# A hybrid RG-LRU, attention and mixture-of-experts layer: an explicit TensorE order in the RG-LRU stage, gates alternating with eighths of a sigmoid block, adaLN sums left in the stage

## The chip, the core and the metric

The kernel runs on one core of one Trainium2 chip. Five engines work side by side and wait for each other by semaphores: TensorE (PE in the rows) multiplies matrices into PSUM, ScalarE (ACT) and VectorE (DVE) work on tiles, GpSimd (POOL) does the same more slowly and starts a few transfers, SyncE (SP) only issues DMA transfers. Each engine runs its own instructions strictly in order. The metric is the device time of one execution in microseconds, as the median of several.

## The reference

One layer for 1024 latent tokens and 256 context tokens, width 1024, in float32. Three branches share one input projection; the part that the change touches is the first.

```python
z_l = split(modulate(rmsnorm(x, g1), mod_l[0], mod_l[1]) @ w_in)      # also z_c from the context
xr  = centred_depthwise_conv(z_l[0], conv_w, conv_b)                  # width 4, per channel
for d, rev in ((0, False), (1, True)):                                # RG-LRU, both directions
    r, i  = sigmoid(xr @ wa[d] + ba[d]), sigmoid(xr @ wx[d] + bx[d])  # block diagonal, 8 blocks
    log_a = -8 * r * softplus(-lam[d])
    h[d]  = scan(exp(log_a), sqrt(-expm1(2 * log_a)) * (i * xr))      # starts from the context's state
rnn = (h[0] + h[1]) * gelu(z_l[1])
g   = sigmoid(z_l[5])                                                 # two gates of 1024 channels
merged = g[0] * (rnn @ w_rnn_out) + g[1] * (attention @ w_mla_out)
x_new  = x + mod_l[2] * (merged @ w_o)
out    = x_new + mod_l[5] * moe(modulate(rmsnorm(x_new, g2), mod_l[3], mod_l[4]))
mod_l  = split(silu(c) @ w_ada + b_ada, 6)                            # the adaLN sums
```

## The kernel before

A float32 product is done as three products of rounded parts (high by high, low by high, high by low), so that each weight and each activation exists as a pair of tiles: `wh`/`wl`, `xh`/`xl`, `xrh`/`xrl`, `rh`/`rl`. ACT casts the high part from the raw tile (`wr`), DVE subtracts for the low part.

The work goes in stages: the norm and the first adaLN sums, the projections for attention, then the **RG-LRU stage** (TensorE from about 265 to 588.5 us in the profiled execution), the product with `w_rnn_out` (tile `ro`), attention, the output projection, routing, and sixteen experts.

The RG-LRU stage goes over 8 blocks of 128 channels. For block b:

- `conv_part(b + 1)`: 48 matmuls of 512 columns (tile `z0`, printed `z` in the rows) and 24 of 256 columns for the context (`z0c`); ACT copies the sums out and DVE adds the three other taps (tile `xr`).
- `lru_part(b)`: four gates (r and i, two directions), each of 6 matmuls of 512 columns (`gz`) and 3 of 256 (`gc`), with ACT's sigmoid on each; then ACT's tanh (`vv`) and, after a load of another function table, exp (`av`). DVE squares (`r`), forms `vv`, and after ACT's square root `i`, then scans (`r`, three instructions), adds the directions and multiplies with the gelu tile (`ge`), which goes to memory (`rn_d`). GpSimd multiplies `i` with `xr`.
- `sig_block`: a block of the merge gates, 48 matmuls (`zg`), ACT's sigmoid (`sg`), and a store. `sig_plan` gives blocks 0 to 7 one, one, one, two, one, one, two and three of them.
- `mod_step`: one of 32 slices of the later adaLN rows. A slice of `w_ada` is loaded into a `wr` buffer and DVE adds it, scaled, into `acc`. Every eighth ends a row: TensorE sums `acc` over the partitions with a matrix of ones (`mp`, 4 matmuls), ACT copies the row (`g`), and it is stored.

In this stage the order of ACT is that of the code (a manual schedule); the orders of TensorE, DVE, GpSimd and SP are set by a scheduler. PSUM is eight banks: tag "a" has three buffers of two banks (`gz`, `z0`, `zg`, `mp`, later `ro`), tag "b" two of one bank (`z0c`, `gc`). `wr` buffers for weights, `w_ada` slices and reloaded `rn_d` rows come from one set of four.

In block 7 the three sig blocks come last. Around them `load_rn` begins to bring back the rows of `rn_d` and to split them (`rh`, `rl`) into memory that the stage's own tiles had held, and `ro` of the next stage multiplies them with `w_rnn_out`: 8 output blocks of 48 matmuls, k from 0 to 7 inside.

Of the kernel before, what the change touches and what calls it, by code (L numbers as in the profile page):

```python
# [19 lines left out]
F32 = mybir.dt.float32  # L20
# [40 lines left out]
def layer_kernel(ctx: ExitStack, tc: tile.TileContext, I, rope_tab, out, dbg=None):  # L61
# [269 lines left out]
    def nextw(shape):  # L331
        n = taken[0]
        assert items[n][1] == shape, (items[n], shape)
        taken[0] = n + LOOK
        fetch()
        taken[0] = n + 1
        return ahead[n]

    LOOK = 2
    NFIRST = 3  # L340
    MP2, N2 = 1, 0
# [38 lines left out]
    cur_pool = []  # L380

    def mpool():
        return cur_pool[-1]

    macc = {}

    def mod_step(j):
        m, k = divmod(j, KD)
        if k == 0:
            macc[m] = mpool().tile([P, D], F32, name="acc", bufs=1)  # L390
            nc.gpsimd.memset(macc[m], 0.0)
            nc.sync.dma_start(macc[m][0:1, :], I["b_ada"][:, (2 + m) * D:(3 + m) * D])
# [4 lines left out]
        if k == KD - 1:  # L397
            row = mpool().tile([1, D], F32, name="g", tag="sg", bufs=1)
            mp = pa("mp")
            for n in range(2):  # L400
                sl = slice(n * 512, (n + 1) * 512)
                nc.tensor.matmul(mp[0:1, sl], ones, acc[:, sl], start=True, stop=True)
            nc.scalar.copy(row, mp[0:1, :])
            nc.sync.dma_start(mod_d[m:m + 1, :], row)


    with pool("p2") as p2:
# [141 lines left out]
        cur_pool.append(p2)  # L549
# [9 lines left out]
        for j, i in enumerate(order):  # L559
            zp = qkv(i, *zp, lambda: zq(order[j + 1]) if j + 1 < len(order) else None)  # L560
            if fill:
                fill_block(*fill.pop(0))
            for _ in range(MP2):
                if steps and steps[0] < N2:
                    mod_step(steps.pop(0))


    p3c = pool("p3")
    p3 = p3c.__enter__()
    if True:  # L570
        p4c = None

        def sig_block(dst, mid=None):
            zz = pa("zg")
            zblock(zz)
# [9 lines left out]
        def conv_part(b):  # L585
            zc, zz = pb("z0c"), pa("z0")
# [8 lines left out]
            xrh = p3.tile([P, TOK], F32R, name="xrh", bufs=2)  # L595
            xrl = p3.tile([P, TOK], F32R, name="xrl", bufs=2)
            return xr, xrh, xrl

        def lru_part(b, xr, xrh, xrl):
            gh, gl_ = nextw([2, 2, P])  # L600
            gates = []
            for d in range(2):
                for g, bn in ((0, "ba"), (1, "bx")):
                    gc, gz = pb("gc"), pa("gz")
# [4 lines left out]
                    r = p3.tile([P, TOK], F32, name=("r", "i")[g], bufs=2)  # L609
# [4 lines left out]
            av, vv = [], []  # L614
            for d in range(2):
                v = p3.tile([P, TOK], F32, name="vv", bufs=2)
                nc.scalar.activation(v, gates[2 * d], AF.Tanh, scale=p8[:, d * 8 + b:d * 8 + b + 1])
                vv.append(v)
            for d in range(2):
# [8 lines left out]
            def rest():  # L628
# [17 lines left out]
                nc.sync.dma_start(rn_d[b], ge)  # L646

            return rest
# [3 lines left out]
        def load_rn(n=None):  # L652
            for k in range(len(rh), n or min(len(rh) + 2, KD - 1)):
# [7 lines left out]
        cur_pool.append(p3)  # L661
        with tc.manual_schedule(engines={mybir.EngineType.Activation}):
# [20 lines left out]
            split(nxt[1], nxt[2], nxt[0])  # L683
            for b in range(KD):
# [3 lines left out]
                rest = lru_part(b, *cur)  # L688
                if b + 1 < KD:
                    split(nxt[1], nxt[2], nxt[0])  # L690
                for n in range(sig_plan[b]):
                    w, bb = jobs.pop(0)
                    if b == KD - 1 and n == 1:
                        assert not steps
# [3 lines left out]
                    sig_block((s0_d, s1_d)[w][bb], rest if n == 0 else load_rn if b == KD - 1 else None)  # L698
                    for _ in range(4):
                        if steps:  # L700
                            mod_step(steps.pop(0))
            load_rn(KD)


    xnp.__exit__(None, None, None)
# [107 lines left out]
    for b in range(KD):  # L813
        h, l = nextw([KD, P])
        po = pa("ro")
        for k in range(KD):
            for n in range(2):
                sl = slice(n * 512, (n + 1) * 512)
                mm3(po[:, sl], h[:, k], l[:, k], rh[k][:, sl], rl[k][:, sl], k == 0, k == KD - 1)
        sg = p4.tile([P, SEQ], F32, name="s0", bufs=1)  # L820
# [460 lines left out]
```

## Time and profile before

| | |
|---|---|
| median of 3 executions | 1780.97 us (1778.66 to 1781.80) |
| profiled execution | 1780.6 us, span 1778.5 us |
| mean granted TensorE clock in it | 0.977 of full speed |
| TensorE busy | 1675.9 us, 94% of the span |
| VectorE busy | 1336.1 us, 75% |
| ScalarE busy | 992.9 us, 56% |

The span runs from the first to the last instruction of the profile; the rest of the execution's time lies around it. "Busy" of TensorE is modelled from the starts of its matmuls and their pipelined ends, so that neighbours overlap; how fast it goes is read from start to start. Idle time stands in brackets behind the instruction that it came before, with what ended it.

### The profile page before, as it was taken

The page shows a single profiled execution, that of the slowest core. Times are in us where ns is not written, and L with a number is a line of the kernel's source. Part 1 is how long each engine was busy: PE and PEld are TensorE (multiplying, and loading weights), DVE is VectorE, ACT ScalarE, POOL GpSimd, SP SyncE. Part 2 cuts the span into 40 slices and gives each one's busy share as a digit, 9 for nine tenths or more (in the row PEclk, how much of TensorE's full clock was granted, in tenths as well). Part 3 has the DMA queues.
Part 4 walks back from the last instruction along what each step waited for, and adds up shares of the span by engine and source line. Part 5 has one row for each costly group of instructions (what it writes and reads, how often), then busy time and mean ns, then how long its engine had stood idle before and what let it go on. Part 6 is the DMA issues. An engine that isn't in the chain of part 4 may idle for free.

```text
span 1778.5 us, 20714 instructions
## 1 busy us (share of the span) xinstructions
PE 1675.9 (94%) x7769; PEld 1345.5 (76%) x7769; DVE 1336.1 (75%) x1628; ACT 992.9 (56%) x1087; POOL 251.8 (14%) x188
## 2 busy tenths in 40 slices
PE   8999999999999999999999899909999999999996
PEld 3788888787777877777677678807888888888885
DVE  5755545898897554787876756687999999989995
ACT  3433325765677313667776532406777777777773
POOL 2123331111221100111110100000121111112101
PEclk9999999999999999999999999958999999999999
DMA  9264444445452854000000446567999999999971
GB/s 345 83 176 107 111 104 116 129 145 174 148 158 95 284 173 162 28 28 28 28 1 0 160 183 228 231 249 265 379 397 392 399 396 385 399 400 378 393 296 24
DMA packets 174179, 363.72 MB, mean 205 GB/s; under 512 B 40160, under 2 KB 90744, under 8 KB 174080
## 3 DMA queue, kind: packets, MB, share of 16 engines
q1 hardware_dynamic: 169472, 345.63, 53.6%
q0 software_dynamic: 4608, 16.78, 3.7%
q8 instruction: 61, 1.00, 0.2%
q14 instruction: 38, 0.31, 0.0%
HBM read 314.84 MB, written 47.54 MB: 204 GB/s over the span
## 4 chain that ended last, share of the span: by engine, by line
PE 63%; DVE 17%; issue 6%; ACT 6%; DMA 5%; POOL 3%; SPq 0%; POOLq 0%; DVEq 0%; ACTq 0%
PE w_e_gate L99 3%; PE w_e_gate L100 3%; PE w_e_gate L98 3%; PE w_e_down L99 3%; PE w_e_down L100 3%; PE w_e_down L98 3%; PE w_e_up L99 3%; PE w_e_up L98 3%; PE w_e_up L100 3%; PE pm L783 2%; POOL st L143 2%; PE xo L98 2%; PE s L98 2%; PE xo L100 2%; PE xo L99 2%
## 5 line engine op out<-in xcount | busy, mean ns | idle before, releaser
L95 DVE TENSOR_TENSOR el<-ma,eh 128x2048 fp32r<-128x2048 f32 x114 | 258.4, 2288 | 24.0 <-PE w_e_down L99 12.6
L94 ACT CAST eh<-ma 128x2048 fp32r<-128x2048 f32 x114 | 217.7, 1914 | 75.4 <-PE w_e_up L100 28.8
L95 DVE TENSOR_TENSOR el<-me,eh 128x2048 fp32r<-128x2048 f32 x78 | 176.9, 2288 | 18.9 <-PE w_e_gate L99 7.2
L94 ACT CAST eh<-me 128x2048 fp32r<-128x2048 f32 x78 | 148.9, 1914 | 49.8 <-PE w_e_gate L100 19.4
L847 ACT ACTIVATE pr<-s 128x512 f32<-128x512 f32 x160 | 95.6, 600 | 75.3 <-PE s L100 73.8
L785 DVE TENSOR_REDUCE mx<-pm 128x1 f32<-128x320 f32 x256 | 114.6, 484 | 23.4 <-PE pm L783 21.0
L99 PE MATMUL z<-xl,wh 128*128 128x512 f32 x320 | 126.6, 396 | 1.7 <-DVE xl L280 1.7
L100 PE MATMUL z<-xh,wl 128*128 128x512 f32 x320 | 126.3, 396 | 0.9 <-POOL wl L326 0.9
L98 PE MATMUL z<-xh,wh 128*128 128x512 f32 x320 | 126.4, 397 | 0.0
L1227 POOL DMA_INDIRECT out_dram<-y,icol x16 | 52.3, 3268 | 471.6 <-DVE y L1226 471.6
L94 ACT CAST wh<-wr 128x1024 fp32r<-128x1024 f32 (+1 forms) x53 | 52.0, 982 | 118.2 <-PE z L99 52.4
L95 DVE TENSOR_TENSOR pl<-pr,ph 128x1024 fp32r<-128x1024 f32 x64 | 81.3, 1271 | 31.5 <-ACT ph L94 24.8
L98 PE MATMUL w_e_gate<-eh,xgh 128*128 128x512 f32 x256 | 102.4, 400 | 1.1 <-ACT xgh L94 1.1
L99 PE MATMUL w_e_gate<-el,xgh 128*128 128x512 f32 x256 | 102.3, 400 | 0.0
L100 PE MATMUL w_e_gate<-eh,xgl 128*128 128x512 f32 x256 | 101.3, 396 | 0.2 <-DVE xgl L95 0.2
L99 PE MATMUL w_e_down<-el,hdh 128*128 128x512 f32 x256 | 101.5, 396 | 0.0
L98 PE MATMUL w_e_down<-eh,hdh 128*128 128x512 f32 x256 | 100.4, 392 | 1.1 <-ACT hdh L94 1.1
L99 PE MATMUL w_e_up<-el,xgh 128*128 128x512 f32 x256 | 100.8, 394 | 0.6 <-DVE el L95 0.6
L100 PE MATMUL w_e_down<-eh,hdl 128*128 128x512 f32 x256 | 100.7, 393 | 0.5 <-DVE hdl L95 0.5
L98 PE MATMUL w_e_up<-eh,xgh 128*128 128x512 f32 x256 | 100.8, 394 | 0.0
L100 PE MATMUL w_e_up<-eh,xgl 128*128 128x512 f32 x256 | 99.9, 390 | 0.0
L783 PE MATMUL pm<-kh,qh 97*128 97x320 f32 x256 | 86.8, 354 | 8.4 <-DVE kl L95 4.0
(337 smaller groups left out, 4326.2 us busy)
## 6 DMA issues: line engine op xcount, KB each, us to landing
ma<-in_w_e_down_dram SPq DMA_DIRECT2D x40, 1024.0 KB, 8.0
ma<-in_w_e_up_dram SPq DMA_DIRECT2D x38, 1024.0 KB, 7.4
ma<-in_w_e_gate_dram SPq DMA_DIRECT2D x36, 1024.0 KB, 9.6
me<-in_w_e_gate_dram SPq DMA_DIRECT2D x28, 1024.0 KB, 10.0
me<-in_w_e_up_dram SPq DMA_DIRECT2D x26, 1024.0 KB, 7.2
me<-in_w_e_down_dram SPq DMA_DIRECT2D x24, 1024.0 KB, 7.7
wr<-in_w_in_dram SPq DMA_DIRECT2D x32, 512.0 KB, 4.8
wr<-in_w_ada_dram SPq DMA_DIRECT2D x32, 512.0 KB, 3.6
```

Source lines behind the costliest of these rows:

```text
L94: nc.scalar.copy(h, src)
L95: nc.vector.tensor_tensor(l, src, h.bitcast(F32), OP.subtract)
L98: nc.tensor.matmul(o, lh, rh, start=start, stop=False)
L99: nc.tensor.matmul(o, lh, rl, start=False, stop=False)
L100: nc.tensor.matmul(o, ll, rh, start=False, stop=stop)
L143: nc.gpsimd.tensor_tensor(ap, ap, h, OP.pow)
L783: nc.tensor.matmul(pm[:, 0:320], qh[:, t * P:(t + 1) * P], kh[:, g * 320:(g + 1) * 320], start=True, stop=True)
L785: nc.vector.tensor_reduce(mx[:, g, t:t + 1], pm[:, 0:320], axis=AX.X, op=OP.max)
L847: nc.scalar.activation(pr[:, sl], sp_, AF.Exp)
L1227: nc.gpsimd.indirect_dma_start(out=out_rows, out_offset=bass.IndirectOffsetOnAxis(ap=icol[:, e:e + 1], axis=0), in_=y, in_offset=None, com ...
```

## The change

TensorE's order in the RG-LRU stage is now that of the code too. The stage has PSUM tiles of its own (`z0c` one bank, `z0`/`zg`/`mp` two buffers of two banks, `gc` one bank, `gz` one buffer of two banks), and the next stage again others. Six matmuls of the block's first sig block follow each gate, the other five eighths follow the fourth; the tanh of a direction stands right after its two gates. Five `mod_step`s stand at a block's end instead of four after each sig block. A finished `acc` waits until the next conv's matmuls are done (`mod_out`), is then summed over the partitions, and the result goes into its own first row and from there to memory. `xrh` and `xrl` have one buffer instead of two, `r` three instead of two, `acc` two instead of one; the sigmoid tile of the last blocks is a tile of its own (`sg4`) instead of a `wr` buffer; `load_rn` brings up to four rows at a time instead of two; the last `rn_d` store is issued by GpSimd. The first two `ro` blocks do k = 0 to 6 one after the other and then k = 7.

```diff
+    def mod_out():
+        while mod_done:
+            m = mod_done.pop()
+            acc = macc[m]
+            row = acc[0:1, :]
+            mp = pz("mp")
...
+    open_psum("ps3")
+    def pz(name):
+        return ps["p"].tile([P, 1024], F32, name=name, tag="z", bufs=2)
...
+        def sig_mm(look=None):
+            zz = pz("zg")
+            h, l = nextw([KD, P], look)
+            for n in range(2):
+                for k in range(0, KD, 2):
+                    zhalf(zz, h, l, n, (k, k + 1))
+                    yield zz
...
-                sg = wst.tile([P, SEQ], F32, name="wr", tag="wr", bufs=4)
+                sg = p4.tile([P, SEQ], F32, name="sg4", bufs=2)
...
-            xrh = p3.tile([P, TOK], F32R, name="xrh", bufs=2)
-            xrl = p3.tile([P, TOK], F32R, name="xrl", bufs=2)
+            xrh = p3.tile([P, TOK], F32R, name="xrh", bufs=1)
+            xrl = p3.tile([P, TOK], F32R, name="xrl", bufs=1)
...
+            zg = sig_mm(1)
             for d in range(2):
                 for g, bn in ((0, "ba"), (1, "bx")):
-                    gc, gz = pb("gc"), pa("gz")
+                    gc = ps["p"].tile([P, 512], F32, name="gc", bufs=1)
+                    gz = ps["p"].tile([P, 1024], F32, name="gz", bufs=1)
...
+                    next(zg)
...
-            for k in range(len(rh), n or min(len(rh) + 2, KD - 1)):
+            for k in range(len(rh), n or min(len(rh) + 4, KD - 1)):
...
-        with tc.manual_schedule(engines={mybir.EngineType.Activation}):
+        with tc.manual_schedule(engines={mybir.EngineType.Activation, mybir.EngineType.PE}):
...
                 if b + 1 < KD:
                     nxt = conv_part(b + 1)
-                rest = lru_part(b, *cur)
+                mod_out()
+                rest, zg = lru_part(b, *cur)
...
-                    for _ in range(4):
-                        if steps:
-                            mod_step(steps.pop(0))
+                for _ in range(5):
+                    if steps:
+                        mod_step(steps.pop(0))
...
+    early = []
+    for b in range(2):
+        early.append((pa("ro"), *nextw([KD, P])))
+        ro_mm(*early[b], range(KD - 1))
```

TensorE, two neighbouring gates of block 7 (`gz` and `gc` are the gate's sums, `zg` the sig block's). Before, a gate is followed by the next gate:

```order
L98 MATMUL gc<-xrh,wh 128x256
L99 MATMUL gc<-xrl,wh 128x256
L100 MATMUL gc<-xrh,wl 128x256
L98 MATMUL gz<-xrh,wh 128x512
L99 MATMUL gz<-xrl,wh 128x512
L100 MATMUL gz<-xrh,wl 128x512
```

With the change, six matmuls of the sig block stand between them:

```order
L98 MATMUL gc<-xrh,wh 128x256
L99 MATMUL gc<-xrl,wh 128x256
L100 MATMUL gc<-xrh,wl 128x256
L98 MATMUL zg<-xh,wh 128x512
L99 MATMUL zg<-xl,wh 128x512
L100 MATMUL zg<-xh,wl 128x512
L98 MATMUL zg<-xh,wh 128x512
L99 MATMUL zg<-xl,wh 128x512
L100 MATMUL zg<-xh,wl 128x512
L98 MATMUL gz<-xrh,wh 128x512
L99 MATMUL gz<-xrl,wh 128x512
L100 MATMUL gz<-xrh,wl 128x512
```

An eighth of the sig block has moved up between the gates; the number of matmuls is the same.

ACT at the end of block 7, from the first sig block's sigmoid on, with buffer numbers (`wh` are casts of `w_rnn_out`, `rh0` to `rh7` the reloaded rows of `rn_d`). Before:

```order
L582 ACTIVATE sg_4476<-zg_4409 128x1024
L94 CAST wh_4486<-wr_4484 128x1024
L94 CAST rh0_4540<-wr_4538 128x1024
L94 CAST rh1_4546<-wr_4544 128x1024
L582 ACTIVATE wr_4550<-zg_4483 128x1024
L94 CAST wh_4556<-wr_4554 128x1024
L94 CAST rh2_4610<-wr_4608 128x1024
L94 CAST rh3_4616<-wr_4614 128x1024
L582 ACTIVATE wr_4620<-zg_4553 128x1024
```

With the change:

```order
L601 ACTIVATE sg_4476<-zg_4350 128x1024
L94 CAST wh_4486<-wr_4484 128x1024
L94 CAST rh0_4540<-wr_4538 128x1024
L94 CAST rh1_4546<-wr_4544 128x1024
L94 CAST rh2_4552<-wr_4550 128x1024
L94 CAST rh3_4558<-wr_4556 128x1024
L601 ACTIVATE sg4_4562<-zg_4483 128x1024
L94 CAST wh_4568<-wr_4566 128x1024
L94 CAST rh4_4622<-wr_4620 128x1024
L94 CAST rh5_4628<-wr_4626 128x1024
L94 CAST rh6_4634<-wr_4632 128x1024
L601 ACTIVATE sg4_4638<-zg_4565 128x1024
```

The last sigmoid, which reads the last sig block out of PSUM, stood behind four casts of `rh` before and stands behind seven now. In the built program the first matmul of `ro` of the changed kernel waits for that sigmoid, since the tile shares a bank with `zg_4565`; before, it had a buffer that an earlier sigmoid had freed.

VectorE in block 7, from the exp's consumer to the gelu product. Before:

```order
L624 SCALAR_TENSOR_TENSOR vv_4395<-r_4350,vv_4395 128x1280
L624 SCALAR_TENSOR_TENSOR vv_4397<-r_4378,vv_4397 128x1280
L95 TENSOR_TENSOR wl_4413<-wr_4410,wh_4412 128x1024
L633 TENSOR_TENSOR i_4364<-i_4364,vv_4395 128x1280
L633 TENSOR_TENSOR i_4392<-i_4392,vv_4397 128x1280
```

With the change:

```order
L650 SCALAR_TENSOR_TENSOR vv_4380<-r_4357,vv_4380 128x1280
L650 SCALAR_TENSOR_TENSOR vv_4422<-r_4399,vv_4422 128x1280
L659 TENSOR_TENSOR i_4377<-i_4377,vv_4380 128x1280
L659 TENSOR_TENSOR i_4419<-i_4419,vv_4422 128x1280
```

One weight split has left this run of instructions; another one, between the scans, stays.

## Rows read from the trace of the kernel before

**Rows 1.** The page, part 1: busy us, share of the span, instructions.

```profile
PE 1675.9 (94%) x7769; PEld 1345.5 (76%) x7769; DVE 1336.1 (75%) x1628; ACT 992.9 (56%) x1087; POOL 251.8 (14%) x188
```

**Rows 2.** Two windows: length, busy PE, PEld, DVE, ACT, POOL, clock, DMA.

```profile
265.00:588.70 323.70, 310.57 (x1466) 251.76 (x1464) 264.99 (x228) 205.64 (x211) 56.04 (x22) 1.00 0.44 139
588.70:688.60 99.90, 98.27 (x461) 80.15 (x461) 45.96 (x72) 22.05 (x26) 5.03 (x8) 1.00 0.63 215
```

**Rows 3.** Waits of TensorE from 290 to 588.7: total, times, longest.

```profile
PE gc L98 <- DVE xr L593: 9.3, 7, 2.3
PE gz L98 <- ACT r L611: 3.8, 6, 0.6
```

**Rows 4.** Timeline of TensorE: start, duration, line, tiles, idle before.

```profile
265.16 0.37 PE L98 MATMUL z0c<-xh,wh 128*128 128x256 f32 x1
...
266.84 0.50 PE L98 MATMUL kv<-ukv,zh 128*128 128x512 f32 x1
...
294.31 0.40 PE L98 MATMUL gz<-xrh,wh 128*128 128x512 f32 x1
...
371.63 0.40 PE L100 MATMUL gz<-xrh,wl 128*128 128x512 f32 x1
373.18 0.38 PE L98 MATMUL gc<-xrh,wh 128*128 128x256 f32 x1 [1.15 <-DVE xr L593]
...
548.85 0.39 PE L98 MATMUL gz<-xrh,wh 128*128 128x512 f32 x1
...
555.78 0.40 PE L98 MATMUL zg<-xh,wh 128*128 128x512 f32 x1
...
588.70 0.50 PE L98 MATMUL ro<-rh,wh 128*128 128x512 f32 x1
```

**Rows 5.** Timeline of VectorE: an adaLN sum at the end of block 3.

```profile
446.55 1.28 DVE L396 SCALAR_TENSOR_TENSOR acc<-wr,sc,acc 128x1024 f32<-128x1024 f32 x1 [7.14 <-DMA wr<-in_w_ada_dram]
```

**Rows 6.** Timeline of ScalarE, block 2 and the end of the stage.

```profile
367.09 1.12 ACT L611 ACTIVATE r<-gz,colv 128x1024 f32<-128x1024 f32 x1
...
555.63 1.12 ACT L611 ACTIVATE i<-gz,colv 128x1024 f32<-128x1024 f32 x1 [0.26 <-PE gz L100]
...
556.99 2.62 ACT L617 ACTIVATE vv<-r,sp 128x1280 f32<-128x1280 f32 x2
...
588.75 1.05 ACT L94 CAST wh<-wr 128x1024 fp32r<-128x1024 f32 x1 [9.96 <-DMA wr<-in_w_rnn_out_dram]
591.19 1.05 ACT L94 CAST rh<-wr 128x1024 fp32r<-128x1024 f32 x1 [1.38 <-DMA wr<-rn_d]
...
593.44 1.03 ACT L582 ACTIVATE wr<-zg 128x1024 f32<-128x1024 f32 x1
```

**Rows 7.** Timeline of VectorE, end of the stage.

```profile
562.31 2.89 DVE L623 TENSOR_TENSOR r<-av 128x1280 f32<-128x1280 f32 x2 [9.73 <-ACT av L622]
...
567.92 1.22 DVE L95 TENSOR_TENSOR wl<-wr,wh 128x1024 fp32r<-128x1024 f32 x1
...
579.94 1.23 DVE L645 TENSOR_TENSOR ge<-ge,r 128x1024 f32<-128x1024 f32 x1
581.08 2.35 DVE L95 TENSOR_TENSOR rl<-wr,rh 128x1024 fp32r<-128x1024 f32 x2
```

**Rows 8.** SP's queue, end of the stage: when transfers were issued.

```profile
582.80 0.40 SPq L321 DMA_DIRECT2D wr<-in_w_rnn_out_dram  x1
...
583.92 2.12 SPq L655 DMA_DIRECT2D wr<-rn_d  x2
```

**Rows 9.** DMA view from 580 to 600: size, median time from issue to landing.

```profile
wr<-rn_d SPq DMA_DIRECT2D x6, 512.0 KB, 3.9
```

**Rows 10.** Windows around two returns to work, columns as in rows 2.

```profile
1204.30:1210.50 6.20, 6.16 (x14) 4.38 (x15) 1.90 (x2) 0.27 (x1) 0.12 (x1) 0.50 0.27 85
...
1023.00:1026.20 3.20, 1.54 (x5) 0.60 (x4) 2.52 (x4) 0.62 (x1) 0.00 (x0) 1.00 1.03 412
1026.20:1029.60 3.40, 3.40 (x9) 2.53 (x9) 1.68 (x4) 0.92 (x3) 0.00 (x0) 0.50 1.00 384
```

More of the change, by code (lines that the diff above doesn't have):

```diff
@@ L337, in nextw, with look_ahead @@
         return ahead[n]
+    def look_ahead():
+        n = taken[0]
+        taken[0] = n - 1 + LOOK
+        fetch()
+        taken[0] = n
     LOOK = 2
     NFIRST = 3
-    MP2, N2 = 1, 0
     def zhalf(dst, h, l, n, ks=range(KD)):
@@ L397, in mod_step @@
         if k == KD - 1:
[L398 to L399 removed]
+            mod_done.append(m)
+    def mod_out():
[4 more added lines that the diff above has]
+            mp = pz("mp")
             for n in range(2):
@@ L585, in conv_part @@
         def conv_part(b):
-            zc, zz = pb("z0c"), pa("z0")
+            zc, zz = ps["p"].tile([P, 512], F32, name="z0c", bufs=1), pz("z0")
             zblock(zz, zc[:, 0:CTX])
@@ L594, in conv_part, with split_xr @@
                                                    xr[:, o + lo:o + hi], op0=OP.mult, op1=OP.add)
-            xrh = p3.tile([P, TOK], F32R, name="xrh", bufs=2)
-            xrl = p3.tile([P, TOK], F32R, name="xrl", bufs=2)
+            return xr
+        def split_xr(xr):
+            xrh = p3.tile([P, TOK], F32R, name="xrh", bufs=1)
+            xrl = p3.tile([P, TOK], F32R, name="xrl", bufs=1)
+            split(xrh, xrl, xr)
             return xr, xrh, xrl
@@ L645, in rest @@
                 nc.vector.tensor_tensor(ge, ge, hf[:, LT], OP.mult)
-                nc.sync.dma_start(rn_d[b], ge)
-            return rest
+                (nc.gpsimd if b == KD - 1 else nc.sync).dma_start(rn_d[b], ge)
+            return rest, zg
         rh, rl = [], []
         def load_rn(n=None):
-            for k in range(len(rh), n or min(len(rh) + 2, KD - 1)):
+            for k in range(len(rh), n or min(len(rh) + 4, KD - 1)):
                 t = wst.tile([P, SEQ], F32, name="wr", tag="wr", bufs=4)
@@ L682, in layer_kernel @@
             nc.vector.tensor_scalar(m8, p_, -8.0, None, op0=OP.mult)
-            split(nxt[1], nxt[2], nxt[0])
+            nxt = split_xr(nxt)
             for b in range(KD):
@@ L812, in layer_kernel, with ro_mm @@
     pre = [f for fs in head_ops(0) for f in fs]
[L813 to L816, printed above, removed]
+    def ro_mm(po, h, l, ks):
+        for k in ks:
             for n in range(2):
@@ L819, in layer_kernel @@
                 mm3(po[:, sl], h[:, k], l[:, k], rh[k][:, sl], rl[k][:, sl], k == 0, k == KD - 1)
+    early = []
+    for b in range(2):
+        early.append((pa("ro"), *nextw([KD, P])))
+        ro_mm(*early[b], range(KD - 1))
+    for b in range(KD):
+        if b < 2:
+            po, h, l = early[b]
+            ro_mm(po, h, l, [KD - 1])
+        else:
+            h, l = nextw([KD, P])
+            po = pa("ro")
+            ro_mm(po, h, l, range(KD))
         sg = p4.tile([P, SEQ], F32, name="s0", bufs=1)
```

37 lines of the change are left out of this document (15 added, 22 removed).

## The prediction

> **What bounds the kernel now.** I read the page first: TensorE is busy for 94% of the span [rows 1], so time can be won only where it waits. The two windows of the stage that changes and of the next one show how much there is: in the 323.7 us of the RG-LRU stage TensorE is busy for 310.6, VectorE for 265.0, at the full clock, and the ro stage behind it is filled with 98.3 of 99.9 us [rows 2]. The view of waits, for TensorE alone, names them: seven waits of a context gate (`gc`) for VectorE's `xr`, which holds the PSUM buffer that `z0c` and `gc` share, 9.3 us in all, and six of a gate (`gz`) for ScalarE's sigmoid, 3.8 us [rows 3]. A wait costs more from start to start than its idle time says: the one at 373.18 has 1.15 us of idle, but its matmul starts 1.55 us after the one before, against 0.23 without a wait, so 1.32 us is lost [rows 4]. With 0.17 more for each, the 13 waits are 13.1 + 2.2 = 15.3 us. From block 0's first gate (294.31) to the first matmul of `ro` (588.70) it is 294.4 us [rows 4], so TensorE's own work there is 279.1 us. No other stage has an edit on its path.
>
> **The change part by part.** All sums run from TensorE's rows; a gain or loss at the first matmul of `ro` goes through to the end one to one, since the ro stage is full.
>
> *Start of the stage.* Before, the scheduler put 13 context matmuls of `z0c` between a transpose and the `kv` product that waits for it: 265.16 to 266.84 [rows 4]. In the code's order they come later and nothing fills this wait: a loss of 1.7 us, so block 0's gates start at 296.0. Bounds: 0 if the wait is already over, 1.7.
>
> *Waits at the gates.* `gc` and `z0c` have a bank each, and nothing between conv and gates reads `gc`'s bank on VectorE: the 9.3 us (10.5 with the 0.17 each) go. `gz` has one buffer, so the second gate waits until ScalarE has read the first; an eighth of the sig block (32.92 us over 24 eighths in block 7, 1.37 us [rows 4]) lies in between. In block 2 ScalarE came to the first gate only at 367.09 and was done at 368.21 [rows 6], because it copies `xr` and casts a weight first; the copies still stand ahead of it. I take for each block what one of the six waits costs today, 3.8/6 + 0.17 = 0.8 us, and half of it in the four blocks where `mp` stands ahead of the gates: 4 x 0.8 + 4 x 0.4 = 4.8. Bounds: 0 and 8 x 0.8 = 6.4. The later gates have an eighth and a gate, 3.1 us, for 1.6 us of sigmoids, and wait for nothing.
>
> *The adaLN sums.* Five slices at a block's end put one more on VectorE in each of the first blocks, and their loads go through the four `wr` buffers. Today one such load already held VectorE for 7.1 us, at 446.55 [rows 5]. Behind the sums stand VectorE's `xr` and the waits that ScalarE's sigmoid `sg` of the block is queued behind; two PSUM buffers serve `z0`, `zg` and `mp` now, so a conv that meets a late `sg` stops TensorE. This can happen once, at the conv ahead of block 5. Bounds: 0, and the 7.1 us of that row; I take 2.5, nearer to nothing, since the stage's VectorE is idle for 59 of 323.7 us [rows 2] and some of that slack lies there. `mp` itself and its row copy are moved, not added.
>
> *So the last sig matmul* ends at 296.0 + 279.1 + 4.8 + 2.5 = 582.4, which is 6.3 us earlier than today. Call this moment L.
>
> *The first matmul of ro.* Today it follows at once, although the last sigmoid, behind four casts of `rh`, runs only at 593.44 [rows 6]: its PSUM buffer was another one. In the changed program it shares a bank with the last sig block and waits for that sigmoid, which now stands behind the casts up to `rh6`. When can they run? The last gate ends three eighths later than in a row of gates; three sig blocks less three eighths, 32.92 - 4.12 = 28.8 us, follow it, so it ends at L - 28.8. From there to VectorE's first `r` is 6.53 us today (555.78 to 562.31 [rows 4, 7]); one tanh, half of the pair's 2.62 [rows 6], has moved ahead and one cast of 1.05 has come in: 6.3, at L - 22.5. From `r` to the end of `ge` is 18.86 us today (562.31 to 581.17 [rows 7]), and one weight split of 1.14 (567.92 to 569.06) has left: `ge` ends at L - 4.8. The memory of `rh3` had held `ge`, and VectorE does `rl0` to `rl3` only behind it, at 1.18 each [rows 7]: 4.7 us. Only then is the buffer free that `rh6`'s row is loaded into. The pair of loads issued at 583.92 reached ScalarE at 591.19, 7.2 us later [rows 6, 8]; the median of the neighbourhood is 3.9 [rows 9]. Ahead of it in the queue stand a load of `w_rnn_out`, two more rows and a store, so it is nearer to the first; I take 6.5. Then the cast, 1.05, and the sigmoid, 1.03 [rows 6]. Together -4.8 + 4.7 + 6.5 + 2.1 = 8.5: `ro` starts at L + 8.5 (5.9 to 9.2), 590.9, 2.2 us later than today. Today's load of `w_rnn_out`, 582.80 to 588.75 [rows 6, 8], shows that transfers there do take about 6 us.
>
> *The clock.* TensorE, which had the full clock all through the stage, comes back from 8.5 us of idle. Where it was busy for only 1.54 of 3.20 us (at 1023) it was granted 0.50 in the 3.40 us after, and after the long pause of routing it ran 6.20 us at 0.50, 14 matmuls in a time for 27 [rows 10]. At 0.50 half of the time is lost: 1.7 or 3.1 us; I take 2.4. [...]
>
> *The rest.* Doing k = 0 to 6 of two `ro` blocks first changes the order of the same 96 matmuls; `rh7`, whose row comes last, gets 84 matmuls, 19 us at 0.23, to arrive. The store of the last `rn_d` row from GpSimd is on that path alone. One buffer for `xrh`/`xrl` makes the next cast wait for the gates, which are done long before it. I cost these at nothing; without the cover of 19 us, `rh7` would add what it is late.
>
> *Sum*: 2.2 + 2.4 = +4.6 us. Against the profiled execution, 1780.6, that is 1785.2; the median of the runs, 1780.97, lies 0.4 above it, so 1785.6.
>
> **The rivals.**
>
> *Faster: the last sigmoid is in time.* If VectorE's chain of block 7 ends 6 us earlier against L than worked out, or a wait of TensorE's in the last sig blocks moves L back by that much, and the loads land in 3.9 us, the sigmoid is read at once: `ro` starts at L, 582.4, -6.3 us at a full clock: 1774.7, and 1772.2 if the conv does not wait either. For it: VectorE is free in block 7, with 9.73 us of idle ahead of `r` [rows 7]. Against: each step from the last gate to `ge` is a chain of instructions whose durations I have rows for. It decides from an idle time under 2.7 us. Chance 0.19.
>
> *No change.* The wait is there but at its lower bound, 5.9 us, the conv does not wait, and the clock costs 1.7: -6.3 - 2.5 + 5.9 + 1.7 = -1.2, 1779.8. Chance 0.27.
>
> *VectorE becomes the bound.* It has 265 us of work in 323.7, and a fifth sum in each of the first six blocks; if every wait taken off the gates comes back as a conv or a sig block that waits for VectorE's `xr` and ScalarE behind it, the 15.3 us stay, L is 590.4, and `ro` starts 10.2 us later: 10.2 + 2.4 = +12.6, 1793.6. For it: the 7.1 us of [rows 5]. Against: the idle 59 us. Chance 0.14.
>
> **How the numbers follow.** The forecast has 0.40. Its own range is from 1781 (no conv wait, idle of 7, clock 1.7) to 1791 (a conv wait of 7.1, idle of 9.2, clock 3.1). A measurement of this kernel tells about 0.2%, 3.6 us, from no change; a third of the forecast's own cases, 0.13, lie within that, besides the 0.27 of no change and little of the last rival. So faster 0.19, same 0.39, slower 0.42. The range for 8 in 10 goes from 1775, which holds the milder half of the faster cases, to 1793.
>
> **What would show it.** In the profile after: no wait of `gc` for `xr`; a wait of about 0.8 us for ScalarE at the second gate of a block; the first gate near 296; the last sig matmul at 578 to 588; then TensorE idle for 6 to 9 us, ended by ScalarE's sigmoid, which follows a cast of `rh6` that waited for its load; `ro` first at 0.50 of the clock; and a ro stage of the same 100 us. The prediction is wrong if `ro` starts without a pause, if the stage keeps its waits under other names, or if the last sig matmul is later than 590.

## The result and the profile after

The changed kernel takes 1793.18 us (1791.41 to 1794.84), the kernel before in the same rounds 1781.38: a ratio of 1.0066, with a 95% interval of [1.0047, 1.0086]. It is slower by 11.8 us. The profiled execution took 1791.4 us with a span of 1789.3; the span grew by 10.8.

The same windows as in [rows 2] come first (length, busy PE, PEld, DVE, ACT, POOL, clock, DMA): the RG-LRU stage up to the first matmul of `ro`, then the `ro` stage in two parts.

```profile
265.00:599.50 334.50, 312.44 (x1466) 254.95 (x1465) 281.34 (x237) 212.54 (x219) 56.66 (x24) 0.98 0.45 146
599.50:606.40 6.90, 6.81 (x24) 6.10 (x25) 2.22 (x6) 1.70 (x3) 1.95 (x3) 0.50 0.99 358
606.40:702.40 96.00, 94.75 (x436) 76.95 (x436) 35.14 (x56) 13.06 (x17) 1.98 (x3) 1.00 0.48 158
```

The RG-LRU stage is 10.8 us longer with the same number of matmuls, and it no longer runs at the full clock throughout. The `ro` stage begins at half speed. The view of TensorE's waits from 290 to 620 (total, times, longest) answers to [rows 3]:

```profile
PE ro L98 <- ACT sg L601: 8.8, 1, 8.8
PE z L98 <- ACT sg L601: 5.3, 1, 5.3
PE zg L100 <- DVE wl L95: 3.7, 2, 3.2
PE gz L98 <- ACT r L637: 2.9, 3, 2.0
```

The seven waits of `gc` for VectorE are gone. In their place stand two long waits in block 3 and one at the stage's end. TensorE's timeline (start, duration, line, tiles, idle before), at the places that answer to [rows 4]:

```profile
266.99 0.50 PE L98 MATMUL kv<-ukv,zh 128*128 128x512 f32 x1 [1.44 <-ACT zh L94]
...
401.66 0.50 PE L100 MATMUL zg<-xh,wl 128*128 128x512 f32 x1 [3.19 <-DVE wl L95]
...
402.65 0.63 PE L100 MATMUL zg<-xh,wl 128*128 128x512 f32 x1
403.08 0.63 PE L98 MATMUL gz<-xrh,wh 128*128 128x512 f32 x1
...
435.40 0.79 PE L98 MATMUL z<-xh,wh 128*128 128x512 f32 x1 [5.33 <-ACT sg L601]
...
590.23 0.39 PE L100 MATMUL zg<-xh,wl 128*128 128x512 f32 x1
...
599.59 0.79 PE L98 MATMUL ro<-rh,wh 128*128 128x512 f32 x1 [8.81 <-ACT sg L601]
```

Read the starts: after the wait at 401.66 a matmul takes 0.43 us from start to start (402.65 to 403.08) where it takes 0.23 at the full clock. Block 0's first gate starts at 296.01 (not shown), as the first term of the prediction had it. The last sig matmul starts at 590.23; with 0.23 for it, L = 590.46. From the first gate to L it is 294.45 us: no shorter than the 294.4 of before. Then comes the pause of 9.1 us.

**Block 3.** VectorE's timeline (idle before, in brackets, with what ended it) and ScalarE's, ahead of the wait at 435.40:

```profile
412.18 1.28 DVE L396 SCALAR_TENSOR_TENSOR acc<-wr,sc,acc 128x1024 f32<-128x1024 f32 x1
416.10 1.56 DVE L396 SCALAR_TENSOR_TENSOR acc<-wr,sc,acc 128x1024 f32<-128x1024 f32 x1 [2.64 <-DMA wr<-in_w_ada_dram]
418.03 1.29 DVE L396 SCALAR_TENSOR_TENSOR acc<-wr,sc,acc 128x1024 f32<-128x1024 f32 x1 [0.36 <-DMA wr<-in_w_ada_dram]
...
421.68 1.28 DVE L396 SCALAR_TENSOR_TENSOR acc<-wr,sc,acc 128x1024 f32<-128x1024 f32 x1 [1.23 <-DMA wr<-in_w_ada_dram]
424.82 1.28 DVE L396 SCALAR_TENSOR_TENSOR acc<-wr,sc,acc 128x1024 f32<-128x1024 f32 x1 [1.85 <-DMA wr<-in_w_ada_dram]
426.02 2.88 DVE L649 TENSOR_TENSOR r<-av 128x1280 f32<-128x1280 f32 x2
```

```profile
417.03 2.62 ACT L648 ACTIVATE av<-r,sp 128x1280 f32<-128x1280 f32 x2
...
430.34 2.67 ACT L658 ACTIVATE vv<-vv 128x1280 f32<-128x1280 f32 x2 [8.23 <-DVE vv L650]
433.03 1.28 ACT L601 ACT_TABLE_LOAD   x1
434.33 1.02 ACT L601 ACTIVATE sg<-zg 128x1024 f32<-128x1024 f32 x1
```

The exp (`av`) is done at 419.65, but VectorE takes it up only at 426.02: five adaLN sums stand ahead in its order, and four of them wait for their loads, 6.1 us together. ScalarE loses 8.2 us behind that, its sigmoid of the sig block comes late, and the conv's `z` has no PSUM buffer until then. It is the chain that the prediction named for its conv wait. This one came behind the sums that stand in block 3, ahead of block 4's gates.

Why the loads came late shows in SP's queue:

```profile
412.29 7.38 SPq L395 DMA_DIRECT2D wr<-in_w_ada_dram  x4
```

The first of these four loads was issued when a weight split had given its `wr` buffer back, the other three each at the moment that an earlier one of the five adds did (413.49, 417.69, 419.34), and they landed 3.8 to 5.4 us after their issue. So the adds and their loads wait for each other through the few buffers that are free.

**The end of the stage**, ScalarE's timeline, which answers to [rows 6]:

```profile
585.96 1.06 ACT L94 CAST rh<-wr 128x1024 fp32r<-128x1024 f32 x1 [4.72 <-DVE ge L671]
586.92 1.01 ACT L601 ACTIVATE sg<-zg 128x1024 f32<-128x1024 f32 x1
592.15 1.04 ACT L94 CAST wh<-wr 128x1024 fp32r<-128x1024 f32 x1 [4.22 <-DMA wr<-in_w_rnn_out_dram]
593.93 1.05 ACT L94 CAST rh<-wr 128x1024 fp32r<-128x1024 f32 x1 [0.74 <-DMA wr<-rn_d]
596.38 2.23 ACT L94 CAST rh<-wr 128x1024 fp32r<-128x1024 f32 x2 [1.40 <-DMA wr<-rn_d]
598.52 1.02 ACT L601 ACTIVATE sg<-zg 128x1024 f32<-128x1024 f32 x1
```

VectorE there, which answers to [rows 7], and SP's queue, which answers to [rows 8]:

```profile
584.70 1.23 DVE L671 TENSOR_TENSOR ge<-ge,r 128x1024 f32<-128x1024 f32 x1
585.84 4.62 DVE L95 TENSOR_TENSOR rl<-wr,rh 128x1024 fp32r<-128x1024 f32 x4
```

```profile
587.08 0.38 SPq L321 DMA_DIRECT2D wr<-in_w_rnn_out_dram  x1
588.22 0.32 SPq L681 DMA_DIRECT2D wr<-rn_d  x1
...
589.36 5.45 SPq L681 DMA_DIRECT2D wr<-rn_d  x3
```

`ge` ends at L - 4.5, the four `rl` at L, the rows issued from 589.36 on reach ScalarE at 596.38, and the sigmoid that frees `ro`'s bank is done at L + 9.1. That is the worked chain (L - 4.8, L - 0.1, 6.5 for the load, L + 8.5), step by step.

**Given back.** From the first `ro` to its last matmul it is 102.4 us instead of 99.4, yet the span is only 10.8 longer, not 13.9. In both kernels TensorE comes into the attention stage from a stretch with waits; before, it then ran at half speed, now it does not. The window of before and that of after at the first `po`, columns as above:

```profile
695.10:698.50 3.40, 3.40 (x9) 1.79 (x7) 2.31 (x4) 2.49 (x5) 0.00 (x0) 0.50 0.95 349
```

```profile
708.00:711.50 3.50, 3.50 (x17) 2.31 (x17) 2.31 (x4) 2.78 (x6) 1.06 (x1) 1.00 1.04 339
```

By the first `xo` 2.8 us are made up, and the rest runs as before. Why the clock stayed up this time no run shows.

### The profile page after: what moved, and what is told of

Its sections match the earlier page's. It is cut to its first block, busy times and chain, and to the rows that moved or that the text cites. A ratio compares the mean times of both kernels' runs of the same rounds, so it can differ in the third digit from the quotient of the medians.

```text
span 1789.3 us, 20710 instructions
## 1 busy us (share of the span) xinstructions
PE 1677.9 (94%) x7769; PEld 1350.2 (75%) x7769; DVE 1343.6 (75%) x1628; ACT 992.7 (55%) x1087; POOL 252.2 (14%) x189
## 4 chain that ended last, share of the span: by engine, by line
PE 64%; DVE 17%; issue 6%; ACT 6%; DMA 4%; POOL 3%; POOLq 0%; DVEq 0%; ACTq 0%
PE w_e_gate L99 3%; PE w_e_gate L100 3%; PE w_e_gate L98 3%; PE w_e_down L99 3%; PE w_e_down L100 3%; PE w_e_down L98 3%; PE w_e_up L99 3%; PE w_e_up L98 3%; PE w_e_up L100 3%; PE pm L810 2%; POOL st L143 2%; PE s L98 2%; PE xo L98 2%; PE xo L100 2%; PE s L99 2%
## 5 line engine op out<-in xcount | busy, mean ns | idle before, releaser
L95 DVE TENSOR_TENSOR el<-ma,eh 128x2048 fp32r<-128x2048 f32 x114 | 258.4, 2287 | 23.9 <-PE w_e_down L99 12.3
L95 DVE TENSOR_TENSOR wl<-wr,wh 128x1024 fp32r<-128x1024 f32 (+1 forms) x53 | 68.3, 1290 | 37.0 <-ACT wh L94 34.1
```

What stands on the lines that cost most here:

```text
L95: nc.vector.tensor_tensor(l, src, h.bitcast(F32), OP.subtract)
```

## The experiments

Two theories stood after the result. The first: the loss has two independent parts, the pause ahead of `ro` and the adaLN sums, which make the stage wait again for what the new order had won. The second: one of them is the other's consequence, and mending one mends both. Ratios are to the kernel before on the same chip in the same rounds, with 95% intervals. In their profiled executions the part ahead of the stage took 1 to 6 us longer (15 in e20's), so lengths count from block 0's first gate, to L ("stage"), and from L to the first `ro` ("pause"). The runs without sums (e4, e8) and with other operands (e5, e12) leave out work or compute other numbers: they measure a part, and are no kernels to use.

| kernel | ratio | stage | pause |
|---|---|---|---|
| after | 1.0066 [1.0047, 1.0086] | 294.45 | 9.1 |
| e1: other bank for `ro` | 1.0054 [1.0038, 1.0071] | 293.5 | 0.3, then 9.4 |
| e7: bank, and `lb` later | 1.0000 [0.9986, 1.0014] | 293.8 | 0 |
| e4: no sums | 0.9990 [0.9978, 1.0003] | 282.2 | 9.1 |
| e8: e7, no sums | 0.9933 [0.9912, 0.9954] | 283.7 | 0 |
| e12: sums without loads | 1.0028 [1.0015, 1.0040] | 287.9 | 9.3 |
| e5: sums of `acc` itself | 1.0050 [1.0036, 1.0065] | 294.1 | 9.1 |
| e9: sums spread | 1.0109 [1.0088, 1.0130] | 302.6 | 12.2 |
| e3: four after each sig block | 1.0045 [1.0031, 1.0059] | 291.2 | 9.4 |
| e14: dealt 4,4,4,4,4,4,8,0 | 1.0059 [1.0040, 1.0079] | 304.2 | 0 |
| e16: own buffers | 1.0085 [1.0070, 1.0100] | 307.1 | 0 |
| e17: e16, dealt as e14 | 1.0081 [1.0061, 1.0101] | 307.7 | 0 |
| e18: e14, last row late | 1.0072 [1.0056, 1.0088] | 310.3 | 0 |
| e19: the same, bank as in after | 1.0087 [1.0064, 1.0109] | 309.8 | 1.3 |
| e20: e18, start as before | 1.0089 [1.0072, 1.0106] | 310.2 | 0 |
| e21: e18, no alternation | 1.0165 [1.0146, 1.0185] | 325.8 | 0 |
| e22: e7, dealt 8,4,4,4,4,4,4,0 | 0.9979 [0.9964, 0.9993] | 292.6 | 0 |
| e23: e7, dealt 6,4,4,4,4,4,6,0 | 1.0033 [1.0020, 1.0047] | 300.3 | 0 |

**The pause: e1, e7.** e1 opens the stage's PSUM set with the three gate tiles, so that `ro`'s first tile lies on the banks of `gz`, which are free.

```diff
     open_psum("ps3")
+    for nm, w in (("z0c", 512), ("gc", 512), ("gz", 1024)):
+        ps["p"].tile([P, w], F32, name=nm, bufs=1)
```

> Only the PSUM banks differ: the stage's gz and gc get the low banks, so that the first ro tile lies where the last gate was and no longer on the last sig block. Theory (the 9.0 us pause is the wait for the last sigmoid and nothing else): the first ro matmul follows the last sig matmul at once, near 590.5; TensorE waits at most 1.5 us inside the first ro block for rh4 to rh6; no 0.50 stretch at the start of the ro stage; total 1793.2 - 9.0 - 1 to 2 of clock + up to 1.5, so 1782 to 1786. Rival (the chain of reloaded rows is what is late, the sigmoid only stands behind it): the pause comes back inside the first ro block as a wait for rh4 to rh6, 5 us or more, total 1788 to 1792.

`ro` starts at once, and TensorE then stands for as long as before. TensorE's timeline in e1:

```profile
595.13 0.51 PE L98 MATMUL ro<-rh,wh 128*128 128x512 f32 x1
605.08 1.25 PE L747 MATMUL lb<-wrt,mc 128*128 128x16 f32 x5 [9.44 <-DVE mc L743]
```

A second wait lay under the first, of about the same length. The router's `lb` matmuls come right behind `ro`'s first matmul in TensorE's order, and need VectorE's `mc`. VectorE's timeline in e1:

```profile
602.51 2.43 DVE L95 TENSOR_TENSOR rl<-wr,rh 128x1024 fp32r<-128x1024 f32 x2 [1.21 <-ACT rh L94]
604.85 0.17 DVE L743 COPY mc<-mc 128x16 f32<-128x16 f32 x1
```

`mc` stands behind the splits of the same late rows. Neither I nor the view of waits, which names one releaser for a wait, had seen it. e7 therefore also moves that block behind the first two `ro` blocks.

```diff
+    for nm, w in (("z0c", 512), ("gc", 512), ("gz", 1024)):
+        ps["p"].tile([P, w], F32, name=nm, bufs=1)
...
-    mc_p = pb("mc")
...
     for b in range(2):
         early.append((pa("ro"), *nextw([KD, P])))
         ro_mm(*early[b], range(KD - 1))
+    mc_p = pb("mc")
...
```

> The other PSUM banks of the run before, and the router's small products (mc, lb) after the first two ro blocks instead of ahead of them. Theory (two waits lie on top of each other at the same place, the last sigmoid and lb's wait for VectorE behind the rl splits; the rows themselves come almost in time): from the last sig matmul to the last ro matmul 100 to 102 us instead of 111.5, at the full clock, total 8 to 10 us under the changed kernel, 1.000 to 1.002 of the kernel before. Rival (the reloaded rows are the limit): the first ro block waits 5 us or more for rh4 to rh6, total 1.003 of before or more.

No pause is left, and the ratio is 1.000: against 1.0066 that is 0.66%, 11.8 us, for the pause and its clock together. The two profiled executions show 9.0 of it: 0.7 in the stage and 8.3 from L to the start of the last `ro` matmul, which takes 103.2 us instead of 111.5, though 100 to 102 were expected (99.7 before). The two waits of block 3 stay. So mending the one does not mend the other, and the second theory falls.

**The sums: e4, e8, e12, e5, e6.** e4 takes the 32 loads and adds out of the changed kernel, e8 out of e7.

```diff
-        raw = wst.tile([P, D], F32, name="wr", tag="wr", bufs=4)
-        nc.sync.dma_start(raw, w_ada[k * P:(k + 1) * P, (2 + m) * D:(3 + m) * D])
-        nc.vector.scalar_tensor_tensor(acc, raw, sc[:, k, 0:1], acc, op0=OP.mult, op1=OP.add)
```

> Leaves out the 32 adaLN slices of the stage, their loads and their sums on VectorE (the later adaLN rows are then b_ada alone); the row sums mp stay. Theory (VectorE's wait for the slices, 26 us, delays block 3 and costs TensorE 3.4 + 5.5 us there): block 4's first gate comes 8 to 9 us earlier than 453.2, the pause before ro stays at 8 to 10 us, total 1783 to 1786. Rival (the alternating order costs the time): the block 3 waits stay, total above 1790.

> As the run with banks and lb moved, and without the 32 adaLN slices (their loads and sums are left out, the rows are b_ada alone). Theory (the two losses are separate and add): first gate to last sig matmul 282 us as in the run without sums, then no pause, total 0.992 to 0.995 of before. Rival (they share a cause, and the pause comes back when the stage is shorter, since the reloaded rows then come later against it): 0.997 to 1.000.

Without sums the stage is 282.2 us, 12.3 shorter. The only waits left in it are four at the second gate, 4.55 us from start to start; so TensorE's own work is 277.6. The pause stays, which rules the second theory out from this side too. In e8 both losses are gone, and the time is 0.67% under that of before. Some 12 us for the pause and 12 for the sums, and they add. How much the sums cost in the kernel before no run shows, since it was not run without them.

e12 keeps 32 adds of the same shape, but from the next block's `xr`, with no loads.

```diff
-        raw = wst.tile([P, D], F32, name="wr", tag="wr", bufs=4)
-        nc.sync.dma_start(raw, w_ada[k * P:(k + 1) * P, (2 + m) * D:(3 + m) * D])
+        raw = nxt_xr[0][:, CTX:]
...
                 if b + 1 < KD:
+                    nxt_xr[0] = nxt
```

> Leaves out the loads of the 32 adaLN slices; VectorE does the same 32 instructions, but on the next block's xr, so that they stay at the block's end, where the change has them (the adaLN rows are then other numbers). The run without loads had let them move into block 0. Theory (the waiting for slices in the four shared buffers is the loss): first gate to last sig matmul 283 to 287 us instead of 294.5, the 9 us pause at ro stays, total 1.000 to 1.002 of before. Rival (VectorE's work is the loss, five sums do not fit into a block): 290 us or more, total 1.004 or more.

Waits of TensorE in e12, and the row of the sums by line (busy, mean ns, idle before):

```profile
PE zg L100 <- DVE wl L95: 3.1, 2, 2.8
PE gz L98 <- ACT r L637: 2.6, 2, 2.0
PE z L98 <- ACT sg L601: 1.6, 1, 1.6
```

```profile
L396 DVE SCALAR_TENSOR_TENSOR acc<-xr,sc,acc 128x1024 f32<-128x1024 f32 x32 | 64.3, 2026 | 0.8
```

The `z` wait falls from 5.3 to 1.6 us; the `zg` wait hardly moves. The stage is 287.9, between what the two expectations had: 6.6 of the 12.3 us go with the loads, and at most 5.7 are VectorE's own time, since here an add takes longer than in the changed kernel. There the row reads:

```profile
L396 DVE SCALAR_TENSOR_TENSOR acc<-wr,sc,acc 128x1024 f32<-128x1024 f32 x32 | 50.9, 1593 | 26.0 <-DMA wr<-in_w_ada_dram 16.1 <-DMA acc<-in_b_ada_dram 9.6
```

e5 was an earlier attempt at the same, with `acc` scaled by itself.

```diff
-        nc.vector.scalar_tensor_tensor(acc, raw, sc[:, k, 0:1], acc, op0=OP.mult, op1=OP.add)
+        nc.vector.scalar_tensor_tensor(acc, acc, sc[:, k, 0:1], acc, op0=OP.mult, op1=OP.add)
```

> Leaves out the loads of the 32 adaLN slices; VectorE does the same 32 instructions on the accumulator itself (the adaLN rows are then wrong numbers of the same size). Theory (it is the waiting for loads, not the sums' 51 us of work): as without the sums, total 1783 to 1787, VectorE's idle ahead of acc under 10 us instead of 26. Rival (VectorE is the bound, five sums a block are too much work): total stays within 2 us of 1793 and TensorE still waits 6 us or more in block 3.

With nothing to wait for, the scheduler moved the sums to the front, where they held the tanh's operand back: 7.5 us at a gate of block 0. From block 1's first gate on the stage is 249.8 us, near the 248.3 of e4. The run says little on loads alone, since it moved the sums too.

e6 puts the five sums at a block's end into the kernel before.

```diff
-                    for _ in range(4):
-                        if steps:
-                            mod_step(steps.pop(0))
+                for _ in range(5):
+                    if steps:
+                        mod_step(steps.pop(0))
```

> The kernel before with one edit of the change alone: five adaLN slices at a block's end instead of four after each sig block; TensorE's order there stays the scheduler's. Theory (five slices in a row, whose loads go through the four wr buffers, hold VectorE ahead of the next block): slower than before by 2 to 8 us, 1783 to 1789, with longer waits of gc for xr. Rival (the place of the sums does not matter, the two PSUM buffers of the new order make it matter): within 1.5 us of 1781.

1.0020 [1.0003, 1.0037], and in its profile the waits of `gc` for `xr` are 15.8 us instead of 9.3 in the run of before, with a stage of 304.0 us instead of 294.4, though the time as a whole shows less of it. So putting five sums at a block's end hurts with the scheduler's order of TensorE too, by about as much as in the written order, where undoing it (e3, below) is worth 0.2% as well. That the written order makes the sums dearer is not shown.

**How to deal them: e9, e3, e14, e23, e22.** If five sums in a row are the trouble, spreading should help. e9 does one sum after each gate and one at the end; e3 does four after each sig block, as before.

```diff
                     gates.append(r)
+                    if steps:
+                        mod_step(steps.pop(0))
...
-                for _ in range(5):
-                    if steps:
-                        mod_step(steps.pop(0))
+                if steps:
+                    mod_step(steps.pop(0))
```

> The changed kernel with its five adaLN slices of a block spread: one after each of the four gates, one at the block's end; all else as in the change. Theory (a row of five waits for loads that pass one by one through the four wr buffers; spread, each finds its slice loaded): first gate to last sig matmul 284 to 290 us instead of 294.5, VectorE's idle ahead of acc under 15 us, total 1.001 to 1.005 of before, the 9 us pause at ro unchanged. Rival (the buffers and not the row of five are the limit): 293 us or more, 1.006.

```diff
-                for _ in range(5):
-                    if steps:
-                        mod_step(steps.pop(0))
+                    for _ in range(4):
+                        if steps:
+                            mod_step(steps.pop(0))
```

> One part undone: four adaLN slices after each sig block, as in the kernel before, eight of them in block 3; all else as in the change. Theory (slices in a row wait for their loads): the waits of TensorE move to where the eight stand and stay as large, first gate to last sig matmul 291 to 297 us, total 1.005 to 1.008 of before. Rival (the fifth slice is the cause): 284 to 288 us, 1.002 to 1.004.

Spreading is worse by 0.43%: VectorE's idle time ahead of sums rises from 26.0 to 38.7 us, since more of them meet a load that is still on its way. That theory fell. e3 is 3.3 us better in the stage: the `zg` wait is gone, as in e4, and the `z` wait unchanged (5.6).

e14, e23 and e22 deal the 32 by hand on top of e7; the digits stand in the table.

```diff
-                for _ in range(5):
-                    if steps:
-                        mod_step(steps.pop(0))
+                for _ in range([4, 4, 4, 4, 4, 4, 8, 0][b]):
+                    mod_step(steps.pop(0))
```

> Banks and lb moved, and the slices dealt out as 4, 4, 4, 4, 4, 4, 8, 0 over the blocks instead of 5 six times and 2; block 6 has a second sig block in which VectorE has time. Theory (the backlog grows by the slices ahead of block 3's r): block 4's first gate 2 to 5 us earlier after block 0's, total 0.996 to 0.999 of before. Rival (the buffers decide, the number does not): 1.000 as without it.

> Banks and lb moved, slices dealt out as 8, 4, 4, 4, 4, 4, 4, 0, the last row sum ahead of block 7's gates as in the change. Theory (what counts is how many slices stand ahead of a block's first r on VectorE; block 0 has 5.5 us of idle there): first gate to last sig matmul 284 to 289 us, total 0.994 to 0.998 of before, faster than both kernels. Rival (block 0's eight delay it as the loadless ones did, by 7 us): 291 us or more, total 0.999 or more.

> As the other, dealt out as 6, 4, 4, 4, 4, 4, 6, 0. Theory: block 0 without a new wait; the six of block 6, which end the last row, make the row sum ahead of block 7's gates wait 5 to 10 us: total 0.998 to 1.003 of before. Rival (six in block 6 fit, only the eight did not): 0.994 to 0.997.

In e14 the way to block 4 is 147.8 us (after 157.2), but the last row's sum over the partitions, in block 7, needs the last slices of block 6. One row of TensorE's waits, of e14:

```profile
PE mp L409 <- issue: 18.2, 1, 18.2
```

In e23 that wait is 13.7 us. With eight in block 0 and none late, e22, it is 1.8. Waits of TensorE in e22:

```profile
PE z L98 <- ACT sg L603: 4.6, 1, 4.6
PE gz L98 <- ACT r L639: 4.3, 5, 2.0
PE mp L409 <- ACT sg L603: 1.8, 1, 1.8
```

The `zg` wait of 3.2 us is gone, and the version is the fastest that does all of the work: 0.9979 [0.9964, 0.9993], 3.4 us by the medians (1782.15 to 1785.56). The interval only just leaves out no change, and this is the best of many variants. The stage, 292.6, is longer than the 284 to 289 that were expected. Its profiled execution was 4 us above its median, with a span only 0.6 us under e7's, so the profile does not show where all of the gain is.

**Buffers: e16, e17.** Are the loads late because weights use the same four `wr` buffers? e16 gives `w_ada` two buffers of its own, on top of e7; the room comes from `r`, which goes back to two. e17 adds e14's dealing.

```diff
-        raw = wst.tile([P, D], F32, name="wr", tag="wr", bufs=4)
+        raw = p3.tile([P, D], F32, name="wa", bufs=2)
...
-                    r = p3.tile([P, TOK], F32, name=("r", "i")[g], bufs=3 - g)
+                    r = p3.tile([P, TOK], F32, name=("r", "i")[g], bufs=2)
```

> Banks and lb moved, five slices a block as in the change, but their loads go into two buffers of their own instead of the four shared with the weights; to make room r has two buffers instead of three, as before the change. Theory (waiting for slices is the loss): VectorE's idle ahead of acc falls from 30 to under 12 us, first gate to last sig matmul 284 to 288 us, total 0.994 to 0.998 of before, which beats both kernels. Rival (VectorE's work): first gate to last sig matmul 291 us or more, total 0.999 to 1.001.

> As the run with own buffers, with the slices dealt out as 4, 4, 4, 4, 4, 4, 8, 0. Theory (waiting): the same as with own buffers alone or up to 2 us less, 0.993 to 0.997. Rival (work): better than own buffers alone by 3 us or more, since only the dealing out relieves VectorE.

In e16 VectorE still idles 33.2 us ahead of sums, so sharing is not what makes the loads late, at least against two own buffers; e17 is no better. One row of the waits of SP's queue in e16 shows that there too most of the loads are issued only when an add gives its buffer back:

```profile
SPq L395 <- DVE acc L396: 48.3, 25, 5.0
```

And the third `r` buffer, which the prediction did not speak of, shows its worth: ScalarE's `r` waits 15.6 us for VectorE to free one, which it never did in the changed kernel. One row of e16's waits of TensorE:

```profile
PE gz L98 <- ACT r L639: 18.3, 8, 4.6
```

More own buffers, and three for `r`, were not tried together.

**The late row: e18, e19, e20.** e18 is e14 with the last `mod_out` after block 7's first sig block; e19 the same without e7's two edits; e20 is e18 with the first conv in the scheduler's order.

```diff
-                mod_out()
+                if b + 1 < KD:
+                    mod_out()
...
                     if b == KD - 1 and n == 1:
+                        mod_out()
```

> Banks and lb moved, slices dealt out as 4, 4, 4, 4, 4, 4, 8, 0, and the last row sum (mp) after block 7's first sig block instead of ahead of its gates. Theory (sums ahead of block 3's r are the first loss, the pause at ro the second; they add): first gate to last sig matmul 284 to 288 us, ro at once, total 0.993 to 0.997 of before, so faster than both kernels. Rival (the eight slices of block 6 come back as a wait in block 7): first gate to last sig matmul 292 us or more, total 0.999 or more.

> The changed kernel with the slices dealt out as 4, 4, 4, 4, 4, 4, 8, 0 and the last row sum late, nothing else: the pause at ro stays. Theory (the losses add): first gate to last sig matmul 284 to 288 us, pause 9 to 10 us, total 0.999 to 1.002 of before. Rival (a shorter stage lengthens the pause, since the reloaded rows do not come earlier): pause over 13 us, 1.003 or more.

```diff
-        with tc.manual_schedule(engines={mybir.EngineType.Activation, mybir.EngineType.PE}):
+        with tc.manual_schedule(engines={mybir.EngineType.Activation}):
             nxt = conv_part(0)
+        with tc.manual_schedule(engines={mybir.EngineType.Activation, mybir.EngineType.PE}):
```

> As the first of these, with the first conv left to the scheduler, so that its context matmuls can fill the wait for the last kv product. Theory: kv's wait of 1.7 us is filled, first gate to last sig matmul the same, total 1 to 2 us under the first run. Rival (the first gates wait for VectorE's xr anyway): same as the first within 1 us.

The wait of `mp` only changes its name: in e18 block 7 waits at `xrl`, `wl`, a gate and a sig block (3.0, 3.1, 4.3 and 6.8 us of idle), because the eight sums stand in VectorE's order whoever reads them. In e19 the stage ends so late that the pause shrinks to 1.3 us. e20's wait at `kv` is still there, so the loss at the start was not undone and its cause stays argued from the order alone.

**Alternation: e21** is e18 without the eighths between the gates.

```diff
-                    next(zg)
```

> As the first of these, with the four gates in a row again and the whole sig block after them; PSUM and all else the same. Theory (with one gz buffer each gate waits for ScalarE's sigmoids of the one before, and the alternation is what covers it): gz waits of 1 to 2 us at three gates of each block, first gate to last sig matmul 20 to 45 us longer than in the first run. Rival (ScalarE keeps pace with gates in a row, the gain came from gc's own bank): less than 8 us longer.

The waits of TensorE in e21 are the clearest rows on the change's main edit:

```profile
PE gz L98 <- ACT r L638: 22.4, 16, 4.3
PE gz L98 <- ACT i L638: 6.2, 8, 0.9
```

24 waits, 28.6 us, where e18 has five of 8.1. The stage is 15.5 us longer than e18's, less than the 20 to 45 that were expected. So alternating does what it is said to do: it hides the sigmoids behind which the single `gz` buffer would stand.

## Why the prediction was wrong

The sign was right (slower), and so was the way in which `ro` would come to wait. The time was 7.6 us too low: the measured one lies 0.2 above the range. Of its three signs of being wrong two came: the stage keeps waits under other names, and the last sig matmul is later than 590. By its own terms, against the profiled execution:

- **Start**, 1.7: block 0's gates were put at 296.0, and start at 296.01.
- **Own work**, 279.1: 277.6 by e4. The 13 waits of before are 15.3 us from start to start, as it had; it left out that the matmul behind each wait starts some 0.1 us late as well, and the 0.25 us between L and `ro`.
- **Waits at the gates**, 4.8: 4.55 in e4, which has nothing else to wait for. But they lie at the second gate of four blocks, one of 2.15 and three of 0.80, not in all eight.
- **The adaLN sums**, 2.5: this step failed. It measured 12.3 (after less e4), 9.8 above. I let them cost one conv wait, near its lower bound, "since the stage's VectorE is idle for 59 of 323.7 us". That share is an average, and no slack stood where the five sums came to stand, with a chain behind them that ends in TensorE's next PSUM buffer. Two waits came (3.36 and 5.49 us from start to start), and each was followed by a stretch at half speed, 1.7 and 2.1 us, which makes 12.65; a few waits of under 1 us and fewer at the gates balance the rest. The upper bound of 7.1 was too low as well: it was one wait's row, with no clock behind it and no second wait.
- **L**, 582.4: 590.46, for that reason (-1.5 - 0.25 + 9.8 = 8.05).
- **The pause**, 8.5: 9.1. Each step came as worked out, but another wait of the same length lay under it (e1), which the prediction did not have. Without the bank the time would have been nearly the same.
- **The clock**, 2.4: 3.0 at `ro`. What it missed is the 3.8 us in block 3, and the gain ahead of attention, part of 2.8.

Added up: +8.1 at L, +0.6, +0.6 and -3.1 after it make 6.2, the +10.8 of span against the predicted +4.6.

The rival that fits best is "VectorE becomes the bound": it put L at 590.4 and the time at 1793.6. It was given 0.14. Its mechanism holds in part: waits for VectorE took back what the gates had won, but by two waits for sums behind loads in one block, not by work that fills VectorE; without the loads half of it is gone (e12).

Windows of the changed kernel on the clock, for those 1.7 and 2.1 us:

```profile
402.00:405.00 3.00, 3.00 (x9) 2.38 (x8) 2.97 (x2) 0.00 (x0) 0.00 (x0) 0.54 0.52 175
435.00:438.00 3.00, 2.60 (x6) 2.12 (x7) 3.00 (x2) 0.86 (x2) 0.00 (x0) 0.50 0.43 175
438.00:441.00 3.00, 3.00 (x11) 2.32 (x11) 3.00 (x4) 1.96 (x2) 0.00 (x0) 0.71 0.05 10
```

From start to start eight matmuls each take 0.20 us more than 0.23, and the edges of the two stretches add 0.1 and 0.5. The granted clock is at its lower level of 1.2 GHz there, right after TensorE stood still. The Trainium skill, "TensorE: Matmul & The Clock Gate", Part 1, says that "the ramp penalty is <1% of a typical kernel span". The trace agrees with the figure: 3.0 + 3.8 = 6.8 us are 0.4%. Small as that is, it is almost twice the 0.2% that a measurement of this kernel tells from no change, and it goes with the waits, so a kernel that trades many short waits for three long ones pays it.

Not settled: whether more buffers for `w_ada` would bring its loads forward (two of their own did not), which dealing of the sums is best, what the sums cost in the kernel before, and the cause of the 1.7 us at the start.

## What to carry to other kernels

An engine's order, once written out, stops at every operand that comes late, so look at each producer's order (here five adds, four of them behind a late load, ahead of a chain of three engines) and not at that producer's idle share. Under a wait that you remove, look for the next one: list everything that the following instructions need and when each is done, since the view of waits names only the last releaser of the first. And price a wait with the half-speed stretch behind it.

## What the runs showed of the hardware

- Waits up to 2.3 us in the stage of before left the granted clock at 1.00 [rows 2, 3]; after the ones of 3.4 and 5.5 us it fell to about half for the next eight or nine matmuls, and after the pause of 9.1 for 6.9 us.
- An add of 128x1024 on VectorE takes 1.28 us by itself and up to about three times that beside GpSimd's multiplication. In the changed kernel five of the 32 took longer, 1.6 to 4.0 us, each while GpSimd multiplied; in e12 it was nine, 3.9 to 4.1 us. So the means are 1593 and 2026 ns.
